# Branch projections of a hybrid decoder block: 512-column products over both parts of y_a and y_b, with the halves added per block

## The chip, the cores and the metric

The kernel runs on one core of one Trainium2 chip. The metric is the device time of one execution in microseconds (us), the median of several runs. A profile of one execution of the kernel before was recorded with it; times below that start at 0 count from the start of that profile's span.

## The reference

One layer of a hybrid decoder block over 256 tokens of width 1024, in float32. Two causal mixers (HGRN2, a gated linear recurrence, and MoBA, block-sparse attention, which with 256 tokens is one block and so plain causal attention) read the same projection of x; each gives an output of 8 heads x 128, y_a and y_b. These are projected by one 1024 x 1024 weight each, gated and summed, and projected once more. A SwiGLU feed-forward of width 2816 follows.

```python
proj = jnp.einsum('bsd,dn->bsn', x, w_in)
...
y_a = rms_norm(o_a, hgrn_norm_w...) * jax.nn.silu(hg...)
y_b = moba_attention(q_b, k_b, mv...)
z_a = jnp.einsum('bsc,cd->bsd', y_a, w_branch_a)
z_b = jnp.einsum('bsc,cd->bsd', y_b, w_branch_b)
g_a, g_b = jnp.split(jax.nn.sigmoid(gate_logits + b_gate), 2, axis=-1)
mixed = jnp.einsum('bsc,cd->bsd', g_a * z_a + g_b * z_b, w_out)
x = layer_norm(DN_ALPHA * x + mixed, ln1_w, ln1_b)
h = jnp.einsum('bsd,df->bsf', x, w_ffn_in)
h_gate, h_up = jnp.split(h, 2, axis=-1)
y = jnp.einsum('bsf,fd->bsd', jax.nn.silu(h_gate) * h_up, w_ffn_down)
return layer_norm(DN_ALPHA * x + y, ln2_w, ln2_b)
```

## The kernel before

**Products in two parts.** Every operand of a large product is split into two parts, each of TensorE's reduced fp32 type (fp32r): a leading part (an ACT copy that rounds, L156 for activations, L179 for weights) and the rest (a DVE subtraction, L157 and L181). A product is the sum of three: leading weights x leading activations, leading weights x rest, rest of weights x leading activations. The fourth is left out.

**Weights.** `plan()` lists 81 tiles of 1 MB in the order of use; `fetch()` gives the next tile as (wh, wl) and keeps three more on the way (`LOOKAHEAD`). Bringing a tile in is one DMA on SP's queue, the ACT cast (L179) and the DVE subtraction (L181). There are four buffers for leading parts (`whi`) and four for rests (`wlo`), so the cast of tile i + 4 waits until tile i has been used.

**Stages in order.** The input projections (hf, hq, hi, hg, gb, ga, mk, mq, mv), with the HGRN2 steps run between them; then `za` (four tiles of w_branch_a), with the attention of heads 4 to 7 between its matmuls; `zb` (four tiles of w_branch_b); `wo` (w_out), whose rows_pass takes the k-rows of m two at a time; the first layer norm with an early piece of the FFN (`fe`); the FFN's gate and up products (`fg`, `fu`); the down product (`wd`); the second layer norm.

**The branch projections.** `feat_pair` computes one weight tile's 256 output features for all 256 tokens into one accumulator (a PSUM tile of 2 x 256 columns from the pool `mm`, which has four). For each of the two 128-feature halves f and each of the eight k it issues three matmuls of 256 columns. One k is one head of y. y_a is held as two tiles, yah and yal; y_b as ybh and ybl. DVE then multiplies the accumulator by the gate (L539 for za; L546 for zb, after which L547 adds both branches and L156/L157 split the sum m into mTh and mTl).

**The attention heads.** `moba_head` is a generator: scores on PE (L487, L488), softmax on DVE and ACT (L491 to L500), then the transposes pt (L504), their copy pT (L506), the value product po (L509, L510), and the split into y_b (L156, L157). `side.step()` before each za tile issues one head's work, `side.drain()` the rest before zb.

**The FFN's form.** `wide_pair` (L686 on) already works with a `Pair`: a layout that keeps, for each k, the leading part and the rest side by side, so that both are one operand of 512 columns. It needs two accumulators per weight tile, one for each f; the left half collects leading x leading and rest x leading, the right half leading x rest. The two halves are then added: an ACT copy of the right half to SBUF (L712), and a DVE add of the left one (L713).

**The order.** Each engine runs its instructions in a fixed order, which a planner makes when the program is built (`schedule_with_timeline_sim=True`): it simulates the engines and takes, of the instructions that are ready in its simulated time, the one that comes first in the program. Only a few stretches (`manual_schedule`), wo and the FFN's early piece among them, keep the written order.

Of the kernel before, what the change touches and what calls it, by code (L numbers as in the profile page):

```python
# [10 lines left out]
F32 = mybir.dt.float32  # L11
F32R = mybir.dt.float32r
# [5 lines left out]
P = 128  # L18
T = 256
NT = T // P  # L20
D = 1024
KC = D // P
H = 8
# [87 lines left out]
def hybrid_layer_kernel(ctx: ExitStack, tc, x, xT, vecs, wts, ln1_w, ln1_b, ln2_w, ln2_b, consts, out):  # L111
    nc = tc.nc
# [6 lines left out]
    sm = pool("sm", 2)  # L119
    klp = pool("klp", 1)  # L120
    mm = pool("mm", 4, space=PSUM)
    aux = pool("aux", 4, space=PSUM)

    def slot(name, dt=F32):
        return big.tile([P, 2048], dt, tag="s8", name=name)
# [4 lines left out]
    class Pair:  # L130
# [6 lines left out]
        def __getitem__(self, key):  # L137
# [5 lines left out]
                ks = slice(k0, k0 + ks.stop - ks.start)  # L143
            return self.parts[i][:, ks, u, ts]

        def both(self, k):
            i, k = divmod(k, KC // 2)
            return self.parts[i][:, k, :, :]
# [6 lines left out]
    def split(dst_h, dst_l, src):  # L155
        nc.scalar.copy(dst_h, src)  # L156
        nc.vector.tensor_sub(dst_l, src, r32(dst_h))  # L157
# [27 lines left out]
    def fetch(ahead=LOOKAHEAD):  # L185
        while state["next"] < len(loads) and len(ready) < 1 + ahead:
            list(stage())
        return ready.pop(0)
# [36 lines left out]
    def feat_pair(name, ah=None, al=None):  # L225
        ah, al = (xTh, xTl) if ah is None else (ah, al)
        wh, wl = fetch()
        ps = mm.tile([P, 2, T], F32, tag="mm", name=name)
        for f in range(2):
            feat_steps(ps[:, f, :], wh, wl, f, ah, al, range(KC))  # L230
        return ps

    def feat_steps(ps, wh, wl, f, ah, al, ks, k0=0):
        wcol = slice(f * P, (f + 1) * P)
# [67 lines left out]
    for j in range(2, 4):  # L302
        ps = feat_pair(f"hf{j}")
# [4 lines left out]
    for j in range(4):  # L308
        ps = feat_pair(f"hq{j}")
        sg = sm.tile([P, 2, T], F32, tag="sg", name=f"sgq{j}")  # L310
        nc.scalar.activation(sg, ps, AF.Sigmoid)
        for f in range(2):
            h = 2 * j + f
# [3 lines left out]

    hv = slot("hv").rearrange("p (t d) -> p t d", t=NT)
    hgs = slot("hgs").rearrange("p (h t) -> p h t", h=H)
    yah = slot("yah", F32R).rearrange("p (h t) -> p h t", h=H)  # L320
    yal = slot("yal", F32R).rearrange("p (h t) -> p h t", h=H)

    def free_view(ap, offset, dims):
        return bass.AP(ap.tensor, ap.offset + offset, [ap.ap[0]] + dims)
# [9 lines left out]
    def hgrn_steps():  # L334
# [8 lines left out]
        for g in range(4):  # L343
            ps = aux.tile([P, 4, P], F32, tag="aux", name=f"sd{g}")
            cs = slice(g * 512, (g + 1) * 512)
# [8 lines left out]
        for l in range(LEVELS):  # L354
# [4 lines left out]
            for g in range(2):  # L359
                ps = aux.tile([P, 4, P], F32, tag="aux", name=f"sc{l}_{g}")  # L360
                for a in range(4):
                    h = 4 * g + a
# [25 lines left out]
        for g in range(2):  # L388
            for u in range(NT):
                ps = aux.tile([P, 4, P], F32, tag="aux", name=f"o{g}{u}")  # L390
                for a in range(4):
                    h = 4 * g + a
                    hd = slice(h * P, (h + 1) * P)
                    if u == 1:
                        nc.tensor.matmul(ps[:, a, :], SL[:, h, :], hv[:, 0, hd], start=True, stop=False)
                    nc.tensor.matmul(ps[:, a, :], SD[:, u, h, :], hv[:, u, hd], start=(u == 0), stop=True)
                sq = sm.tile([P, 4, P], F32, tag="sg", name=f"sq{g}{u}")
                nc.scalar.activation(sq, ps, AF.Square)
                st = sm.tile([P, 12], F32, tag="ost", name=f"ost{g}{u}")
                nc.vector.reduce_sum(st[:, 0:4], sq, axis=mybir.AxisListType.X)  # L400
                nc.vector.tensor_scalar(st[:, 4:8], st[:, 0:4], 1.0 / P, RMS_EPS, op0=ALU.mult, op1=ALU.add)
                nc.gpsimd.tensor_tensor(st[:, 8:12], st[:, 4:8], half, op=ALU.pow)
                dst = on[:, u, g * 512:(g + 1) * 512].rearrange("p (a d) -> p a d", a=4)
                nc.vector.tensor_tensor(dst, ps, st[:, 8:12, None].to_broadcast([P, 4, P]), op=ALU.mult)
            yield
            for j in range(2):
                h0 = 4 * g + 2 * j
                pt = aux.tile([P, 2, T], F32, tag="aux", name=f"ot{g}{j}")
                for a in range(2):
                    for u in range(NT):  # L410
                        hd = slice((h0 + a) * P, (h0 + a + 1) * P)
                        nc.tensor.transpose(pt[:, a, u * P:(u + 1) * P], on[:, u, hd], ident)
                ya = sm.tile([P, 2, T], F32, tag="sg", name=f"ya{g}{j}")
                nc.vector.tensor_mul(ya, pt, hgs[:, h0:h0 + 2, :])
                split(yah[:, h0:h0 + 2, :], yal[:, h0:h0 + 2, :], ya)
        yield

    class Steps:
# [49 lines left out]
    qT = slot("qT").rearrange("p (h t) -> p h t", h=H)  # L468
    kT = slot("kT").rearrange("p (h t) -> p h t", h=H)
    mv = slot("mv").rearrange("p (t d) -> p t d", t=NT)  # L470
    ybh = slot("ybh", F32R).rearrange("p (h t) -> p h t", h=H)
    ybl = slot("ybl", F32R).rearrange("p (h t) -> p h t", h=H)

    def rope_pair(nm, dst, j):
        ps = feat_pair(f"m{nm}{j}")
# [9 lines left out]
    def moba_head(h):  # L485
# [9 lines left out]
        p = s  # L495
# [12 lines left out]
        po = aux.tile([P, T], F32, tag="aux", name=f"po{h}")  # L508
        nc.tensor.matmul(po, mv[:, 0, hd], pT[:, 0:T], start=True, stop=False)  # L509
        nc.tensor.matmul(po[:, P:T], mv[:, 1, hd], pT[:, 2 * P:3 * P], start=False, stop=True)  # L510
        split(ybh[:, h, :], ybl[:, h, :], po)
        yield

    def moba_heads(h0):
# [19 lines left out]

    for j in range(4):
        side.step()
        ps = feat_pair(f"za{j}", yah, yal)
        cs = slice(2 * j, 2 * j + 2)
        nc.vector.tensor_mul(ga[:, cs, :], ps, ga[:, cs, :])  # L539
    side.drain()  # L540
    mTh = slot("mTh", F32R).rearrange("p (k t) -> p k t", k=KC)
    mTl = slot("mTl", F32R).rearrange("p (k t) -> p k t", k=KC)
    for j in range(4):
        ps = feat_pair(f"zb{j}", ybh, ybl)
        cs = slice(2 * j, 2 * j + 2)
        nc.vector.tensor_mul(gb[:, cs, :], ps, gb[:, cs, :])  # L546
        nc.vector.tensor_add(ga[:, cs, :], ga[:, cs, :], gb[:, cs, :])  # L547
        split(mTh[:, cs, :], mTl[:, cs, :], ga[:, cs, :])

# [136 lines left out]
    e[1][1].transpose()  # L686


    def wide_pair(name, p, tag):


        wh, wl = fetch()
        pss = []
        for f in range(2):
            ps = p.tile([P, 2, T], F32, tag=tag, name=f"{name}{f}")
            wcol = slice(f * P, (f + 1) * P)
            for k in range(KC):
                nc.tensor.matmul(ps, wh[:, k, wcol], x1p.both(k), start=(k == 0), stop=False)  # L698
                nc.tensor.matmul(ps[:, 0, :], wl[:, k, wcol], x1p[0, k, slice(0, T)],  # L699
                                 start=False, stop=(k == KC - 1))  # L700
            pss.append(ps)
        return pss

    room = slot("room").rearrange("p (i f t) -> p i f t", i=4, f=2)
    for j in range(EARLY, NF, 2):
        n = j // 2 % 2
        sums = []
        for i, (nm, p, tag) in enumerate([("g", mm, "mm"), ("u", aux, "aux")]):
            pss = wide_pair(f"f{nm}{j}", p, tag)
            s = room[:, 2 * i + n, :, :]  # L710
            for f, ps in enumerate(pss):
                nc.scalar.copy(s[:, f, :], ps[:, 1, :])  # L712
                nc.vector.tensor_add(s[:, f, :], ps[:, 0, :], s[:, f, :])  # L713
            if i == 0:
                nc.scalar.activation(s, s, AF.Silu)
            sums.append(s)
        nc.vector.tensor_mul(sums[0], sums[0], sums[1])
        i, k = divmod(j, KC)
        split(ah[i][:, k:k + 2, :], al[i][:, k:k + 2, :], sums[0])
# [46 lines left out]
```

## Time and profile before

| | |
|---|---|
| time, median of 3 runs | 513.84 us (513.62 to 514.0) |
| time of the profiled execution | 513.88 us |
| its span, first to last instruction | 511.8 us |
| mean granted TensorE clock | 0.998 |
| za matmuls: 64 each of L237, L238, L239 | mean 285, 288, 288 ns |
| zb matmuls: 64 each of L237, L238, L239 | mean 285, 283, 284 ns |
| weight cast L179 and subtraction L181 of one za tile | 1.90 and 2.29 us |
| HBM traffic over the span | 178 GB/s |

A row of a timeline gives the start in us from the span's start, the duration in us, the engine, the line of the kernel, the operation, what it writes and reads, the shapes, a count, and in brackets how long the engine had been idle before it and what ended that. PE is TensorE's matmul, PEld its weight load, DVE VectorE, ACT ScalarE, POOL GpSimd, SP the queue that issues the weights' DMAs. Matmuls overlap, so the duration of a row (0.28 us for 256 columns) is longer than the distance between the starts of two rows (0.12 us); where a stream's price is wanted, distances between starts are used. A row of a group gives the count, total busy time, the mean in ns, and the idle time before it.

### The profile page before, as it was taken

The page shows a single profiled execution, that of the slowest core. Times are in us where ns is not written, and L with a number is a line of the kernel's source. Part 1 is how long each engine was busy: PE and PEld are TensorE (multiplying, and loading weights), DVE is VectorE, ACT ScalarE, POOL GpSimd, SP SyncE. Part 2 cuts the span into 40 slices and gives each one's busy share as a digit, 9 for nine tenths or more (in the row PEclk, how much of TensorE's full clock was granted, in tenths as well). Part 3 has the DMA queues.
Part 4 walks back from the last instruction along what each step waited for, and adds up shares of the span by engine and source line. Part 5 has one row for each costly group of instructions (what it writes and reads, how often), then busy time and mean ns, then how long its engine had stood idle before and what let it go on. Part 6 is the DMA issues. An engine that isn't in the chain of part 4 may idle for free.

```text
span 511.8 us, 8120 instructions
## 1 busy us (share of the span) xinstructions
PE 501.4 (98%) x3440; PEld 467.3 (91%) x3440; DVE 338.5 (66%) x387; ACT 249.1 (49%) x303; POOL 39.9 (8%) x33
## 2 busy tenths in 40 slices
PE   8999999999999999999999999999999999999994
PEld 7899889999999998998999988998888888888884
DVE  5677799997565454776764799555756665643436
ACT  6695354444355445566552553444656556434300
POOL 0000000000020063352010000000000000000000
PEclk9999999999999999999999999999999999999999
DMA  7978544343424445543567276147555455437002
GB/s 247 374 280 311 184 172 158 106 150 156 165 83 165 167 169 197 198 161 118 227 214 279 104 269 239 48 165 246 166 193 218 165 181 218 178 122 257 32 1 82
DMA packets 15571, 91.70 MB, mean 179 GB/s; under 512 B 1840, under 2 KB 2864, under 8 KB 5552
## 3 DMA queue, kind: packets, MB, share of 16 engines
q1 hardware_dynamic: 14688, 88.04, 47.4%
q0 software_dynamic: 848, 3.15, 1.8%
q8 instruction: 27, 0.44, 0.3%
q14 instruction: 8, 0.07, 0.0%
HBM read 90.13 MB, written 1.05 MB: 178 GB/s over the span
## 4 chain that ended last, share of the span: by engine, by line
PE 94%; DMA 3%; DVE 1%; SPq 1%; ACT 0%; issue 0%; DVEq 0%
PE fg L698 6%; PE fu L698 6%; PE wd L567 4%; PE wd L566 4%; PE wd L568 4%; PE fu L699 3%; PE fg L699 3%; DMA raw<-in_wts_dram 3%; PE sc L363 3%; PE mk L239 2%; PE hq L239 2%; PE hq L238 2%; PE hq L237 2%; PE zb L239 2%; PE za L239 2%; PE mk L238 2%
## 5 line engine op out<-in xcount | busy, mean ns | idle before, releaser
L181 DVE TENSOR_TENSOR wl<-raw,wh 128x2048 fp32r<-128x2048 f32 (+2 forms) x88 | 186.5, 2122 | 121.1 <-ACT wh L179 120.8
L179 ACT CAST wh<-raw 128x2048 fp32r<-128x2048 f32 (+2 forms) x88 | 155.8, 1774 | 147.9 <-PE wd L568 18.4
L698 PE MATMUL fg<-x1p,wh 128*128 128x512 f32 x144 | 50.4, 392 | 0.0
L698 PE MATMUL fu<-x1p,wh 128*128 128x512 f32 x144 | 50.4, 392 | 0.0
L699 PE MATMUL fg<-x1p,wl 128*128 128x256 f32 x144 | 40.3, 280 | 0.0
L699 PE MATMUL fu<-x1p,wl 128*128 128x256 f32 x144 | 40.3, 280 | 0.0
L567 PE MATMUL wd<-wl,ah 128*128 128x512 f32 (+1 forms) x110 | 38.2, 348 | 0.0
L568 PE MATMUL wd<-wh,al 128*128 128x512 f32 (+1 forms) x110 | 38.1, 347 | 0.0
L566 PE MATMUL wd<-wh,ah 128*128 128x512 f32 (+1 forms) x110 | 38.0, 347 | 0.0
L698 PEld LDWEIGHTS fg<-x1p,wh 128*128 128x128 f32 x144 | 26.9, 187 | 5.9
L698 PEld LDWEIGHTS fu<-x1p,wh 128*128 128x128 f32 x144 | 26.9, 187 | 5.9
L699 PEld LDWEIGHTS fg<-x1p,wl 128*128 128x128 f32 x144 | 27.2, 189 | 0.0
L699 PEld LDWEIGHTS fu<-x1p,wl 128*128 128x128 f32 x144 | 27.2, 189 | 0.0
L566 PEld LDWEIGHTS wd<-wh,ah 128*128 128x128 f32 x110 | 20.8, 189 | 2.8
L568 PEld LDWEIGHTS wd<-wh,al 128*128 128x128 f32 x110 | 20.8, 189 | 2.6
L567 PEld LDWEIGHTS wd<-wl,ah 128*128 128x128 f32 x110 | 20.8, 189 | 2.5
L239 PE MATMUL hf<-xTh,wl 128*128 128x256 f32 x64 | 18.6, 291 | 1.4 <-DVE wl L181 1.3
L237 PE MATMUL hf<-xTh,wh 128*128 128x256 f32 x64 | 18.3, 286 | 0.9 <-ACT wh L179 0.9
L239 PE MATMUL za<-yah,wl 128*128 128x256 f32 x64 | 18.5, 288 | 0.0
L238 PE MATMUL za<-yal,wh 128*128 128x256 f32 x64 | 18.4, 288 | 0.0
L237 PE MATMUL hg<-xTh,wh 128*128 128x256 f32 x64 | 18.4, 288 | 0.0
L237 PE MATMUL mk<-xTh,wh 128*128 128x256 f32 x64 | 18.3, 286 | 0.0
(218 smaller groups left out, 1387.5 us busy)
## 6 DMA issues: line engine op xcount, KB each, us to landing
raw<-in_wts_dram SPq DMA_DIRECT2D x78, 1024.0 KB, 4.8
raw<-in_wts_dram SPq DMA_DIRECT2D x8, 256.0 KB, 4.7
xTr<-in_xT_dram SPq DMA_DIRECT2D x8, 128.0 KB, 4.6
raw<-in_wts_dram SPq DMA_DIRECT2D x2, 512.0 KB, 6.4
xr<-in_x_dram POOLq DMA_DIRECT2D x1, 1024.0 KB, 5.4
wb<-in_ln_w_dram POOLq DMA_DIRECT2D x2, 512.0 KB, 6.0
wb<-in_ln_b_dram POOLq DMA_DIRECT2D x2, 512.0 KB, 7.9
out_dram<-y SPq DMA_DIRECT2D x4, 256.0 KB, 2.1
```

Of the source, the lines that this page charges most:

```text
L179: nc.scalar.copy(h[:, ks, :], raw[:, ks, :])
L181: eng.tensor_sub(l[:, ks, :], raw[:, ks, :], r32(h[:, ks, :]))
L237: nc.tensor.matmul(ps, wh[:, k, wcol], ah[:, kk, :], start=(kk == 0), stop=False)
L238: nc.tensor.matmul(ps, wh[:, k, wcol], al[:, kk, :], start=False, stop=False)
L239: nc.tensor.matmul(ps, wl[:, k, wcol], ah[:, kk, :], start=False, stop=(kk == KC - 1))
L363: nc.tensor.matmul(ps[:, a, :], KL[:, h, :], later(Qt, n, h, 1), start=True, stop=True)
L566: nc.tensor.matmul(ps, lh(kk)[:, ts], wh[:, k, ns], start=(kk == 0), stop=False)
L567: nc.tensor.matmul(ps, lh(kk)[:, ts], wl[:, k, ns], start=False, stop=False)
L568: nc.tensor.matmul(ps, ll(kk)[:, ts], wh[:, k, ns], start=False, stop=(kk == ktot - 1))
L698: nc.tensor.matmul(ps, wh[:, k, wcol], x1p.both(k), start=(k == 0), stop=False)
L699: nc.tensor.matmul(ps[:, 0, :], wl[:, k, wcol], x1p[0, k, slice(0, T)], start=False, stop=(k == KC - 1))
```

## The change

y_a and y_b are held as `Pair`s (yap, ybp), and the za and zb loops use `wide_pair`, which now takes its operand as an argument and stands with the other helpers. For each half f and each k there is one matmul of 512 columns (leading weights, both parts) and one of 256 (rest of weights, leading part) in place of three of 256. The two halves of each accumulator are added by `add_halves` into a new SBUF tile z (pool `sm`, tag `sg`, two buffers), and the multiply by the gate reads z. The FFN's use of these helpers computes what it did.

```diff
+        def split(self, ks, src):
+            split(self[0, ks, slice(0, T)], self[1, ks, slice(0, T)], src)
...
+    def wide_pair(name, a, p, tag):
+        wh, wl = fetch()
+        pss = []
+        for f in range(2):
+            ps = p.tile([P, 2, T], F32, tag=tag, name=f"{name}{f}")
+            wcol = slice(f * P, (f + 1) * P)
+            for k in range(KC):
+                nc.tensor.matmul(ps, wh[:, k, wcol], a.both(k), start=(k == 0), stop=False)
+                nc.tensor.matmul(ps[:, 0, :], wl[:, k, wcol], a[0, k, slice(0, T)],
+                                 start=False, stop=(k == KC - 1))
+            pss.append(ps)
+        return pss
+
+    def add_halves(s, pss):
+        for f, ps in enumerate(pss):
+            nc.scalar.copy(s[:, f, :], ps[:, 1, :])
+            nc.vector.tensor_add(s[:, f, :], ps[:, 0, :], s[:, f, :])
...
-    yah = slot("yah", F32R).rearrange("p (h t) -> p h t", h=H)
-    yal = slot("yal", F32R).rearrange("p (h t) -> p h t", h=H)
+    yap = Pair("yap")
...
-                split(yah[:, h0:h0 + 2, :], yal[:, h0:h0 + 2, :], ya)
+                yap.split(slice(h0, h0 + 2), ya)
...
-    ybh = slot("ybh", F32R).rearrange("p (h t) -> p h t", h=H)
-    ybl = slot("ybl", F32R).rearrange("p (h t) -> p h t", h=H)
+    ybp = Pair("ybp")
...
-        split(ybh[:, h, :], ybl[:, h, :], po)
+        ybp.split(h, po)
...
-        ps = feat_pair(f"za{j}", yah, yal)
+        pss = wide_pair(f"za{j}", yap, mm, "mm")
+        z = sm.tile([P, 2, T], F32, tag="sg", name=f"za{j}")
+        add_halves(z, pss)
         cs = slice(2 * j, 2 * j + 2)
-        nc.vector.tensor_mul(ga[:, cs, :], ps, ga[:, cs, :])
+        nc.vector.tensor_mul(ga[:, cs, :], z, ga[:, cs, :])
...
-        ps = feat_pair(f"zb{j}", ybh, ybl)
+        pss = wide_pair(f"zb{j}", ybp, mm, "mm")
+        z = sm.tile([P, 2, T], F32, tag="sg", name=f"zb{j}")
+        add_halves(z, pss)
         cs = slice(2 * j, 2 * j + 2)
-        nc.vector.tensor_mul(gb[:, cs, :], ps, gb[:, cs, :])
+        nc.vector.tensor_mul(gb[:, cs, :], z, gb[:, cs, :])
...
-            pss = wide_pair(f"f{nm}{j}", p, tag)
+            pss = wide_pair(f"f{nm}{j}", x1p, p, tag)
-            for f, ps in enumerate(pss):
-                nc.scalar.copy(s[:, f, :], ps[:, 1, :])
-                nc.vector.tensor_add(s[:, f, :], ps[:, 0, :], s[:, f, :])
+            add_halves(s, pss)
```

More of the change, by code (lines that the diff above doesn't have):

```diff
@@ L686, in hybrid_layer_kernel @@
     e[1][1].transpose()
[L689 to L702, printed above, removed]
     room = slot("room").rearrange("p (i f t) -> p i f t", i=4, f=2)
```

## The prediction

> **What bounds the kernel now.** I read the page first (engines, then the chain of waits), then the busy time in stretches around the two branch projections, then the timelines of PE, DVE and ACT there.
>
> ```profile
> span 511.8 us, 8120 instructions
> PE 501.4 (98%) x3440; PEld 467.3 (91%) x3440; DVE 338.5 (66%) x387; ACT 249.1 (49%) x303; POOL 39.9 (8%) x33
> PE 94%; DMA 3%; DVE 1%; SPq 1%; ACT 0%; issue 0%; DVEq 0%
> ```
>
> PE is busy for 98% of the span, and 94% of the chain that ended last is PE. The profiled execution took 513.88 us by the clock, 2.1 us more than its span; the median of the three runs is 513.84, so what I take off the one I take off the other. The stretches (columns: length, then PE, PEld, DVE, ACT, POOL busy) are za with its attention heads, zb waiting for the last head, zb closing, and the first half of wo:
>
> ```profile
> 243.00:272.35 29.35, 29.35 (x236) 28.84 (x235) 19.11 (x38) 14.16 (x28) 3.13 (x5) 1.00 0.67 236
> 272.35:284.60 12.25, 12.25 (x104) 12.20 (x103) 3.74 (x4) 2.93 (x5) 0.00 (x0) 1.00 0.51 196
> 284.60:302.00 17.40, 17.40 (x125) 16.44 (x124) 16.55 (x17) 12.35 (x10) 0.00 (x0) 1.00 0.51 185
> 302.00:319.00 17.00, 17.00 (x80) 14.17 (x80) 16.29 (x17) 5.96 (x5) 1.00 (x1) 1.00 0.68 251
> ```
>
> PE has no gap in any of them, at a granted clock of 1.00. So time is won here only if the same sums need less PE time, and lost only if PE gets a gap it doesn't have. DVE is no reserve everywhere: 16.55 of 17.40 us while zb closes, but 3.74 of 12.25 just before.
>
> **The PE stream, removed and added.** A k-step of one 128-column half is three matmuls of 256 columns before, and one of 512 plus one of 256 after. The kernel already runs the second form in its FFN (L698, L699, moving x1p), with the same kinds of operands. Two uninterrupted stretches of the PE timeline:
>
> ```profile
> 246.87 0.28 PE L237 MATMUL za<-yah,wh 128*128 128x256 f32 x1
> 254.42 0.28 PE L237 MATMUL za<-yah,wh 128*128 128x256 f32 x1
> ...
> 355.95 0.39 PE L698 MATMUL fu<-x1p,wh 128*128 128x512 f32 x1
> 373.28 0.39 PE L698 MATMUL fu<-x1p,wh 128*128 128x512 f32 x1
> ```
>
> The first two rows are 21 steps apart: 7.55 / 21 = 0.3595 us a step. The last two are 50 steps apart: 17.33 / 50 = 0.3466. A step becomes 0.0129 us cheaper. There are 8 weight tiles x 2 halves x 8 k = 128 steps, so 1.65 us of PE disappear, half in za and half in zb. That is the whole of the gain, 0.32% of the time; a third of the weight loads goes too, but they ran beside the matmuls and are inside the two step prices.
>
> Here a rule of the Trainium skill speaks against the change. TensorE: Matmul & The Clock Gate, section Back-to-back issue gap, gives a warm matmul N/2.4 ns plus a fixed 2.5 ns; by it three matmuls of 256 are an estimated 327.5 ns and 512 plus 256 an estimated 325.0, so the 128 steps would save 0.32 us in place of 1.65. The trace differs from it (359.5 and 346.6 ns), and the trace decides.
>
> **The evacuation, added.** Each of the 16 accumulators gets an ACT copy of one half and a DVE add; the final multiply then reads z in place of the accumulator. The nearest rows are the same two instructions in the FFN, and multiplies with and without an accumulator operand:
>
> ```profile
> L712 ACT COPY room<-fg x18: 358/369/378, 346.6 to 440.0; 128x256 f32<-128x256 f32 x18
> L713 DVE TENSOR_TENSOR room<-fg,room x18: 412/416/418, 348.3 to 442.3; 128x256 f32<-128x256 f32 x18
> L546 DVE TENSOR_TENSOR gb<-zb,gb 128x512 f32<-128x512 f32 x4 | 2.7, 684 | 5.6 <-PE zb L239 5.6
> L547 DVE TENSOR_TENSOR ga<-ga,gb 128x512 f32<-128x512 f32 x4 | 2.8, 688 | 0.1
> ```
>
> So ACT gains 16 x 0.369 = 5.9 us and DVE 16 x 0.416 = 6.7 us, half in each projection, and the multiply stays at about 0.69. In za this lies beside PE: 3.3 us on a DVE that is free for 29.35 - 19.11 = 10.2 us, 3.0 on an ACT free for 15.2. It costs nothing while the accumulators come free in time. They come from a pool of four, and a tile now takes two where it took one, so an accumulator is needed again after one and a half tiles, 24 steps or 8.3 us, where before it was more than three tiles. In the FFN the interval from the last matmul to the end of the add, where neither engine is held up, is short:
>
> ```profile
> 354.44 0.28 PE L699 MATMUL fu<-x1p,wl 128*128 128x256 f32 x1
> 354.76 0.37 ACT L712 COPY room<-fu 128x256 f32<-128x256 f32 x1 [0.27 <-PE fu L699]
> 355.17 0.42 DVE L713 TENSOR_TENSOR room<-fu,room 128x256 f32<-128x256 f32 x1 [1.01 <-ACT room L712]
> ```
>
> That is 1.15 us. A weight cast of 1.9 us and a wl subtraction of 2.3 us queued ahead (rows below) make it 5.4, still under 8.3. A copy that waits for PE's tile holds up what is behind it on ACT (exps and pT copies of the heads, the next cast), and an add what is behind it on DVE (the heads' softmax, the next wl); PE waits for none of these soon, since casts run three tiles ahead. I cost za at nothing; without that cover it would be the excess over 8.3 us per tile.
>
> **The last head, moved.** The zb tiles run their steps for heads 0 to 6 while head 7 is still in its softmax. These rows follow head 7, from its transposes to the first use and the first finished tile:
>
> ```profile
> 272.35 0.28 PE L237 MATMUL zb<-ybh,wh 128*128 128x256 f32 x1
> 273.30 0.27 PE L504 MATMUL pt<-cst,ms 128*128 128x128 f32 x1
> 274.38 0.48 ACT L506 COPY pT<-pt 128x384 f32<-128x384 f32 x1
> 277.35 0.38 PE L509 MATMUL po<-pT,mv 128*128 128x256 f32 x1
> 278.61 0.42 DVE L157 TENSOR_TENSOR ybl<-po,ybh 128x256 fp32r<-128x256 f32 x1 [1.79 <-ACT ybh L156]
> 280.87 0.40 PE L237 MATMUL zb<-ybh,wh 128*128 128x256 f32 x2
> 284.55 1.91 ACT L179 CAST wh<-raw 128x2048 fp32r<-128x2048 f32 x1 [5.98 <-PE zb L238]
> 284.68 0.69 DVE L546 TENSOR_TENSOR gb<-zb,gb 128x512 f32<-128x512 f32 x1 [5.64 <-PE zb L239]
> ```
>
> zb starts at 272.35, head 7's y_b is split by 279.03, its wide partner k = 7 first runs at 280.87, and zb0 is only finished at 284.6: the planner, which fixes each engine's order when the program is built, has put some 30 steps of four zb tiles in front. After the change the pool holds two zb tiles, so only 2 x 14 = 28 steps can be done without head 7: 28 x 0.3466 = 9.70 us, about 10.7 with the transposes and value products of head 7 among them. Head 7 needs 279.03 - 272.35 = 6.68 us of that, and the cover is 4 us longer. What changes is the order: zb0 and zb1 now close one right after the other, at about 271.5 (272.35 less za's share) + 10.7 + 4 x 0.35 = 283.6, and zb2 can start only when zb0's first half has been copied and added, 1.15 us after the start of its last matmul. That matmul starts near 282.7, the add ends near 283.9. The bounds of this wait are 0 (head 7 closes zb0 earlier, as the data would allow) and 1.15; I take 0.1, by these rows.
>
> **The handover to wo.** After zb the rows of m = ga + gb are split and read by wo at once:
>
> ```profile
> 298.42 2.29 DVE L181 TENSOR_TENSOR wl<-raw,wh 128x2048 fp32r<-128x2048 f32 x1 [0.30 <-ACT wh L179]
> 300.63 1.29 DVE L157 TENSOR_TENSOR mTl<-ga,mTh 128x512 fp32r<-128x512 f32 x2
> 292.71 0.68 DVE L546 TENSOR_TENSOR gb<-zb,gb 128x512 f32<-128x512 f32 x1
> 296.35 0.40 PE L566 MATMUL wo<-wh,mTh 128*128 128x512 f32 x1
> 302.27 0.39 PE L568 MATMUL wo<-wh,mTl 128*128 128x512 f32 x1
> 304.99 0.39 PE L568 MATMUL wo<-wh,mTl 128*128 128x512 f32 x1
> ```
>
> The last two mTl are ready at 301.3 and 301.92; PE reads them at 302.27 and 304.99, so the slack is 1.0 and 3.1 us. The change puts 8 x 0.416 = 3.3 us more on DVE, wo starts 1.5 us earlier, and DVE's closing work starts 1.7 us earlier (283.0 for 284.68) or more: up to 3.1 us of slack goes. The later mTl then just holds; the earlier one holds only if it isn't queued behind the last wl, as it was. Bounds: 0 and 2.1 us. I take 0, because zb2 now closes near 289.4 where its multiply ran at 292.7, so its part is ready in time for the planner to place it ahead of that wl; and what PE consumes first is planned first.
>
> Weights, DMAs and the queues of SP and POOL are unchanged in number and order; the Pair layout takes two slots for y_a and two for y_b as the four tiles before did. The 1.65 us reach the end, since everything behind is the same PE stream.
>
> **The sum.** 513.88 - 1.65 + 0.1 = 512.3 us.
>
> **The rivals.** *DVE is late at wo.* For it: 16.55 of 17.40 us of DVE are taken in that stretch, and the earlier mTl stood behind a wl of 2.29. Against it: 8.5 us of idle DVE just before, which zb0's and zb1's adds can use. With 1.5 us of the 2.1 lost, 513.9 - 0.15 = 513.7, no measurable change.
>
> *PE runs out of open accumulators, slower.* Place: the end of head 7. Before, four open zb tiles covered it; now two. If the planner puts head 7's transposes and value product behind the 28 steps, or if za3 frees its pair late and only zb0's 14 steps (4.85 us) are there, PE waits for the round itself: 273.30 to 274.86 for transposes and copy, 277.35 to 279.03 for product and split, 1.56 + 1.68 = 3.24 us. Time: 513.88 - 1.65 + 3.24 = 515.5, and up to 516.6 with the 1.15 of the evacuation. It decides from the point where head 7 slips by more than the 4 us of cover; the added copies and adds sit on the engines that its softmax needs. Against it: the chain has only to keep its place, and value product and split stood 13 steps into zb.
>
> *Only columns count.* A step moves 768 columns before and after; if the FFN's 0.3466 owes its advantage to something else than the form (its operands, its place), nothing is saved: 513.9. The rule above would give 513.6 here. Against it: both stretches run at the full clock, without gaps, and each is long.
>
> **How the numbers follow.** A measurement of this kernel can tell about 0.2%, 1.03 us, from no change; so faster means under 512.8, slower over 514.9. My forecast (all stalls together under 0.6 us, 511.9 to 512.8) gets 0.54; DVE late at wo 0.20; accumulators run out 0.17; only columns 0.04; 0.05 is for a better case, with fewer switches between heads and projections, down to 511.7, and for mixtures, half of it faster. Faster: 0.54 + 0.03 = 0.57. Same: 0.20 + 0.04 + 0.01 = 0.25. Slower: 0.17 + 0.01 = 0.18. The range goes from 511.7 to 515.0: its upper end takes in the late wo (at its bound 514.3) and small shortages of accumulators, and leaves out most of that case. Signs are mixed, so the likeliest case's own range, 511.9 to 512.8, stands beside it.
>
> **What would show it.** Right: steps of za and zb at 0.347 us; 16 new copies of 0.37 and adds of 0.42; PE without a gap from 243 to 319; wo starting about 1.5 us earlier, near 294.9. Wrong: steps near 0.36 (only columns); in the list of waits, PE zb waiting for ybl or for an add in add_halves, near 277 to 285 (accumulators); PE wo waiting for mTl or wl near 300 (DVE). A shift of the same size with the FFN and later stages changed in length would mean that something outside these steps moved.

## The result, and the profile after

The changed kernel takes 519.86 us (median of 4 runs, 518.73 to 521.26) against 513.73 us before (4 runs): a ratio of 1.0119 [1.0105, 1.0134]. It is 6.1 us slower, where 512.3 was forecast; it lies above the range's 515.0 and above the slow rival's 516.6. One execution of a_za (617.8 us) and one of n_swap (1757.6 us), two experiments below, fell in a slow state and are left out of their times.

The profiled execution took 518.73 us, the shortest of the four. First its page and the four new lines in the list of PE's waits (total, times, longest, in us):

```profile
span 516.4 us, 7895 instructions
PE 502.1 (97%) x3312; PEld 461.1 (89%) x3312; DVE 343.7 (67%) x403; ACT 253.9 (49%) x319; POOL 39.8 (8%) x33
```

```profile
PE wo L593 <- DVE mTl L160: 1.8, 1, 1.8
PE wo L591 <- ACT mTh L159: 1.5, 1, 1.5
PE zb L245 <- DVE ybp L160: 0.9, 1, 0.9
PE zb L245 <- DVE zb L254: 0.9, 1, 0.9
```

There are 128 fewer matmuls, yet PE's busy sum rises by 0.7 us, in part because a row that stands behind a gap is drawn longer (0.50 us for 0.39 in the rows below); so a stream is better judged by its stages and by distances between starts. The stages by the starts of their first matmuls:

| stage | before, us | after, us | difference |
|---|---|---|---|
| za, with heads | 243.11 to 272.35: 29.24 | 242.16 to 269.65: 27.49 | -1.75 |
| zb | to 296.35: 24.00 | to 296.46: 26.81 | +2.81 |
| wo | to 319.03: 22.68 | to 323.57: 27.11 | +4.43 |

Together that is +5.49. The stages behind them kept their lengths, and za began 0.95 us earlier (the first stage, hf, waited 1.3 us for wl before, and did not in this execution). That leaves the 4.6 us by which the span grew; the median is 1.1 us above this execution, and no other execution has a profile. The two first rows of the table are not the worth of the form alone: head 6's transposes and value product, in za before, stand in zb now (273.14 and 276.28), which moves about 0.9 us from one row to the other. The same stretches of the windows view (length, then PE, PEld, DVE, ACT, POOL) show that PE now has gaps:

```profile
242.00:269.65 27.65, 27.65 (x165) 24.46 (x163) 20.09 (x40) 14.89 (x29) 3.04 (x5) 1.00 0.56 200
269.65:283.00 13.35, 12.43 (x75) 10.81 (x74) 5.38 (x12) 4.76 (x10) 0.00 (x0) 1.00 0.72 283
283.00:296.50 13.50, 12.58 (x72) 10.67 (x72) 11.57 (x14) 8.55 (x12) 0.00 (x0) 1.00 0.47 160
296.50:323.60 27.10, 23.81 (x107) 18.50 (x106) 24.02 (x29) 13.21 (x11) 1.00 (x1) 1.00 0.52 195
```

The granted clock is 1.00 in all four, and za has no gap. Its step is what was forecast: 20 steps from one row to the other, 6.94 / 20 = 0.347 us.

```profile
247.28 0.39 PE L245 MATMUL za<-yap,wh 128*128 128x512 f32 x1
254.22 0.39 PE L245 MATMUL za<-yap,wh 128*128 128x512 f32 x1
```

From here on a *gap* is how much later a matmul starts than the one ahead of it and the stream's usual distance (0.12 us behind 256 columns, 0.23 behind 512) would have it. Between 242 and 335 us the gaps of over 0.12 us add up to 0.36 us before and 6.4 after. Four rows hold 5.7 of them (1.09, 1.07, 1.92 and 1.65 us, at 282.49, 288.03, 304.62 and 308.67). Here are these and two others, picked from PE's timeline:

```profile
281.18 0.38 PE L531 MATMUL po<-pT,mv 128*128 128x128 f32 x2
282.49 0.50 PE L245 MATMUL zb<-ybp,wh 128*128 128x512 f32 x1 [0.92 <-DVE ybp L160]
284.03 0.51 PE L245 MATMUL zb<-ybp,wh 128*128 128x512 f32 x1
288.03 0.50 PE L245 MATMUL zb<-ybp,wh 128*128 128x512 f32 x1 [0.92 <-DVE zb L254]
304.62 0.50 PE L593 MATMUL wo<-wh,mTl 128*128 128x512 f32 x1 [1.75 <-DVE mTl L160]
308.67 0.50 PE L591 MATMUL wo<-wh,mTh 128*128 128x512 f32 x1 [1.50 <-ACT mTh L159]
```

The first is for head 7: its value product (po) stands right ahead of the k = 7 steps that need it, and all 28 covering steps have been run by then. One reason why head 7 is late is seen on DVE. In the changed kernel the subtraction of a weight tile stands ahead of head 7's first softmax step (second fence), before it stood behind (first fence). The next subtraction (271.67) then also comes ahead of its last softmax steps (274.94), where before only that of 267.62 did (270.02):

```profile
264.13 0.56 DVE L491 TENSOR_TENSOR ms<-s,cst 128x384 f32<-128x384 f32 x1 [1.27 <-PE s L488]
267.62 2.29 DVE L181 TENSOR_TENSOR wl<-raw,wh 128x2048 fp32r<-128x2048 f32 x1 [0.89 <-ACT wh L179]
```

```profile
264.81 2.29 DVE L184 TENSOR_TENSOR wl<-raw,wh 128x2048 fp32r<-128x2048 f32 x1 [2.12 <-ACT wh L182]
267.43 0.54 DVE L512 TENSOR_TENSOR ms<-s,cst 128x384 f32<-128x384 f32 x1
```

The second is for an accumulator. After the four k = 7 steps that close zb0 and zb1, zb2 starts at 284.03 in zb0's first accumulator, whose add ends at 283.97. Eight steps later it needs zb0's second one:

```profile
283.41 1.91 ACT L182 CAST wh<-raw 128x2048 fp32r<-128x2048 f32 x1
285.22 0.64 ACT L253 COPY zb<-zb 128x256 f32<-128x256 f32 x2
285.35 2.29 DVE L184 TENSOR_TENSOR wl<-raw,wh 128x2048 fp32r<-128x2048 f32 x1 [1.38 <-ACT wh L182]
287.56 0.75 DVE L254 TENSOR_TENSOR zb<-zb,zb 128x256 f32<-128x256 f32 x2
```

Its last matmul starts at 283.18, but its copy stands behind a cast and its add behind a subtraction, so it is free only near 288.0.

For wo (the third and the fourth gap), follow the last zb tile, whose matmuls end near 296.8. First ACT, then DVE:

```profile
296.59 3.72 ACT L182 CAST wh<-raw 128x2048 fp32r<-128x2048 f32 x2 [1.79 <-issue]
300.22 0.35 ACT L253 COPY zb<-zb 128x256 f32<-128x256 f32 x1
```

```profile
298.53 2.29 DVE L184 TENSOR_TENSOR wl<-raw,wh 128x2048 fp32r<-128x2048 f32 x1 [0.29 <-ACT wh L182]
300.74 0.68 DVE L572 TENSOR_TENSOR ga<-ga,gb 128x512 f32<-128x512 f32 x1
301.35 2.28 DVE L184 TENSOR_TENSOR wl<-raw,wh 128x2048 fp32r<-128x2048 f32 x1
303.55 0.41 DVE L254 TENSOR_TENSOR zb<-zb,zb 128x256 f32<-128x256 f32 x1
303.88 0.68 DVE L160 TENSOR_TENSOR mTl<-ga,mTh 128x512 fp32r<-128x512 f32 x1
304.48 0.68 DVE L571 TENSOR_TENSOR gb<-zb,gb 128x512 f32<-128x512 f32 x1
305.08 2.28 DVE L184 TENSOR_TENSOR wl<-raw,wh 128x2048 fp32r<-128x2048 f32 x1
307.29 0.68 DVE L572 TENSOR_TENSOR ga<-ga,gb 128x512 f32<-128x512 f32 x1
308.65 0.69 DVE L160 TENSOR_TENSOR mTl<-ga,mTh 128x512 fp32r<-128x512 f32 x1 [0.68 <-ACT mTh L159]
```

A copy of 0.35 us stands behind two casts (3.72 us). Its add stands behind two subtractions, the multiply behind the add, and the sum behind a third subtraction. That is the second wait of wo; the first is for zb2's mTl, at 303.88. Before, the chain was one multiply straight from the accumulator, and both last mTl were made at 300.63, ahead of two subtractions:

```profile
296.71 0.68 DVE L546 TENSOR_TENSOR gb<-zb,gb 128x512 f32<-128x512 f32 x1
301.84 4.49 DVE L181 TENSOR_TENSOR wl<-raw,wh 128x2048 fp32r<-128x2048 f32 x2
```

Now the first stands behind two and the second behind three.

### The profile page after: what moved, and what is told of

It reads as the page before. It is cut to its first block, busy times and chain, and to the rows that moved or that the text cites. A ratio compares the mean times of both kernels' runs of the same rounds, so it can differ in the third digit from the quotient of the medians.

```text
span 516.4 us, 7895 instructions
## 1 busy us (share of the span) xinstructions
PE 502.1 (97%) x3312; PEld 461.1 (89%) x3312; DVE 343.7 (67%) x403; ACT 253.9 (49%) x319; POOL 39.8 (8%) x33
## 4 chain that ended last, share of the span: by engine, by line
PE 94%; DVE 2%; issue 1%; ACT 1%; DMA 1%; DVEq 0%; SPq 0%
PE fu L245 6%; PE fg L245 6%; PE wd L592 4%; PE wd L593 4%; PE wd L591 4%; PE fu L246 3%; PE fg L246 3%; PE za L245 3%; PE sc L385 3%; PE zb L245 2%; PE hf L260 2%; PE hf L262 2%; PE hf L261 2%; PE mk L262 1%; PE hq L262 1%; PE hq L261 1%
## 5 line engine op out<-in xcount | busy, mean ns | idle before, releaser
L245 PE MATMUL zb<-ybp,wh 128*128 128x512 f32 x64 | 23.1, 403 | 1.8 <-DVE ybp L160 0.9
L245 PE MATMUL za<-yap,wh 128*128 128x512 f32 x64 | 22.9, 400 | 0.0
L261 PE MATMUL hf<-xTl,wh 128*128 128x256 f32 x64 | 18.7, 292 | 0.0
```

Of the source, the lines that this page charges most:

```text
L245: nc.tensor.matmul(ps, wh[:, k, wcol], a.both(k), start=(k == 0), stop=False)
L261: nc.tensor.matmul(ps, wh[:, k, wcol], al[:, kk, :], start=False, stop=False)
```

## The experiments

The theories, as the expectations number them. **1**: the loss lies in zb and at the handover to wo, from two accumulators per tile and from where copies, adds and weights stand in the order; **1a**: it is the order, not the amount. **2**: the extra ACT and DVE work costs time wherever it stands. **3**: copies and adds in za delay the heads. **4**: the hop over ACT, behind the casts. **5**: the adds, on a nearly full DVE. Unless said otherwise the data computed are those of the reference. "Narrow" is the form of before, three matmuls of 256 columns into one accumulator, reading the `Pair` layout.

### One projection at a time

```diff
 a_za, in the zb loop (b_zb: the same in the za loop)
-        pss = wide_pair(f"zb{j}", ybp, mm, "mm")
-        z = sm.tile([P, 2, T], F32, tag="sg", name=f"zb{j}")
-        add_halves(z, pss)
+        z = narrow_pair(f"zb{j}", ybp)
```

> Only za in the new form; zb goes back to three products of 256 columns per step with one accumulator per tile (from the Pair layout). Theory 1 (the 1.65 us of PE are won, half in za; all that is lost is lost in zb and at the handover to wo, through two accumulators per zb tile and through the order of copies, adds and weight work on ACT and DVE): about 0.8 us faster than before, 513.0, no wait of PE between 240 and 320. Theory 2 (the extra ACT and DVE work costs wherever it is, because it delays heads and weights): about half of the 6.1 us of loss, 516.8. Theory 3 (the head chain is delayed by the copies and adds in za, and PE waits for head 7): a PE wait for y_b near 281 remains, 514.

> Only zb in the new form; za with three products of 256 columns per step. Theory 1: the whole loss of the changed kernel and no gain from za, 519.9 + 0.8 = 520.7, with the same waits of PE in wo for mTl and mTh. Theory 2: half of the loss, 516.8. Theory 3: the PE wait for y_b near 281 is gone, the waits in wo stay, 519.8.

a_za took 515.22 us, 1.0028 [1.0018, 1.0038]; b_zb 520.26, 1.0117 [1.0097, 1.0138], before being 513.84. zb alone makes the whole loss, within the noise (about 1.6 us of b_zb's profile are due to a lower clock, see the last section). But za alone doesn't bring its 0.8 us either, although za itself has no gap: the loss is found later, in the waits of a_za:

```profile
PE wo L602 <- DVE mTl L160: 0.6, 2, 0.4
PE zb L257 <- ACT ybp L159: 0.5, 1, 0.5
```

Head 7 is late even for narrow zb tiles, so its delay comes from za (theory 3); the subtraction stands ahead of its first softmax step here too (265.22, then 267.83). In b_zb the wait for ybp is gone, as it should be, and those for the add, mTl and mTh are there (gaps of 1.12, 1.92 and 1.67).

### Without the evacuation, and with half of it

In d_noadd the multiply reads the left half of each accumulator, and the right half is left out of the sum. In e_copies the copies are made and not read. In g_adds there are no copies, and each add takes a constant table in place of the right half.

```diff
 d_noadd
-        z = sm.tile([P, 2, T], F32, tag="sg", name=f"zb{j}")
-        add_halves(z, pss)
-        nc.vector.tensor_mul(gb[:, cs, :], z, gb[:, cs, :])
+        for f in range(2):
+            c = 2 * j + f
+            nc.vector.tensor_mul(gb[:, c, :], pss[f][:, 0, :], gb[:, c, :])
 e_copies: as d_noadd, but with z, and ahead of each multiply
+            nc.scalar.copy(z[:, f, :], pss[f][:, 1, :])
 g_adds: as after, but in place of add_halves
+            nc.vector.tensor_add(z[:, f, :], pss[f][:, 0, :], cos)
```

> The whole change without the evacuation by halves: the gates multiply the left half of each accumulator directly, two multiplies of 256 columns for one of 512; the right half (leading weights x rest of y) is left out of the sum, and there are no copies and no adds. The matmuls and the two accumulators per tile are as in the change. Theory 1: what is left is the PE saving and at most the wait for head 7 (0.9): 512.1 to 513.0. If two accumulators per tile alone were the cause, the two waits in zb (about 2 us) would stay: 514. If the wide form in these loops were slower on PE itself: 516 or more.

> The whole change with its 16 ACT copies but without its DVE adds: the gates multiply the left half of each accumulator directly, as in d_noadd, and the copies of the right halves go to z, which nothing reads; so leading weights x rest of y is left out of the sum. Theory 4 (the hop over ACT is what costs: a copy stands behind a cast of 1.9 us on ACT, and the accumulator and DVE's next step wait for it): most of the loss is back, 517 to 519, with PE waiting for mTh or mTl in wo. Theory 5 (the adds cost, 16 x 0.42 us more on a DVE that is nearly full while zb closes): no loss, as d_noadd, 512.3.

> The whole change with its 16 DVE adds but without its ACT copies: each add takes the left half of the accumulator and a constant table in SBUF; the right half is left out of the sum and nothing waits for ACT. Theory 4: no loss, 512.3 to 513. Theory 5: the loss is back, 517 to 519, with PE waiting for mTl in wo.

| | us | ratio to before | over d_noadd | gaps, us |
|---|---|---|---|---|
| d_noadd | 512.27 | 0.9966 [0.9954, 0.9979] | | 0.36 |
| g_adds | 514.17 | 1.0009 [0.9999, 1.0018] | +1.9 | 1.64 |
| e_copies | 517.64 | 1.0070 [1.0055, 1.0085] | +5.4 | 4.65 |
| after | 519.86 | 1.0119 [1.0105, 1.0134] | +7.6 | 6.4 |

This separates the terms. d_noadd has the 512-column stream and two accumulators per tile, and it is 1.57 us faster than before: the saving is real and of the forecast size, and two accumulators per tile cost nothing while they are read straight away. In the windows of zb and wo PE has no gap:

```profile
269.65:283.00 13.35, 13.35 (x80) 11.74 (x79) 4.50 (x9) 4.12 (x8) 0.15 (x1) 1.00 0.80 301
283.00:296.50 13.50, 13.50 (x78) 11.82 (x77) 13.22 (x17) 7.99 (x6) 0.00 (x0) 1.00 0.50 171
296.50:323.60 27.10, 27.10 (x148) 23.52 (x147) 24.85 (x29) 10.17 (x9) 2.00 (x2) 1.00 0.59 226
```

DVE is busier here than in the changed kernel (13.22 for 11.57 us while zb closes), so a nearly full DVE alone makes no gap; but it leaves little room for the adds. The copies cost more than the adds although they are 5.9 us of an engine that is half idle. They are not read, and yet each multiply stands behind its copy: in e_copies' trace the first one in zb starts at 283.79, after the copy of 283.38, where d_noadd's starts as soon as its matmul is done. So e_copies measures the hop, not only 16 short copies. With the copies alone, zb waits twice and wo waits for mTl (gaps 1.08, 1.08, 1.57, 0.55). Two of the theories are thus each part of it, the hop over ACT (4) the larger.

### Another order

c_late moves the preparation of two FFN weight tiles behind the first layer norm. i_tail writes zb2 and zb3 into the stretch whose order is kept as written. f_aux takes zb2's accumulators from the other pool.

```diff
 c_late
-        prefetch(2)
         norm1(0)
+        prefetch(2)
 i_tail, at the head of the manual_schedule stretch
+        for j in range(2, 4):
+            branch_b(j)
 f_aux
-        pss = wide_pair(f"zb{j}", ybp, mm, "mm")
+        pss = wide_pair(f"zb{j}", ybp, *((aux, "aux") if j == 2 else (mm, "mm")))
```

> The whole change, and the two FFN tiles that are brought in during the first half of wo are brought in after the first layer norm's DVE work in the written order, so that two casts and two wl subtractions no longer stand ahead of the last copies, adds and splits of zb. Theory 1a (the order, not the amount, of the ACT and DVE work makes PE wait in wo): the waits for mTl and mTh, 3.3 us and their restarts, about 4.0, go: 516. Theory 2 (DVE has too much to do there in any order): the amount is the same, PE still waits in wo, or the layer norm and the FFN's first tile come late: 519 or more.

> The whole change, all sums as in it; the last two zb tiles stand inside the stretch that keeps the written order, ahead of the weights of wo and the FFN, so that ACT makes their copies before the casts that follow in the text, and DVE their adds before the wl subtractions. Theory 1a (the order makes PE wait in wo, 3.64 us of extra distance between starts plus restarts, and the FFN's weights have time): the waits in wo go and none appears in fe, unlike in c_late; the two waits in zb (1.09 and 1.07) stay: 519.9 - 4.2 = 515.7. Theory 2 (too much for DVE in any order): PE waits in wo or fe for as long as before, 519 or more.

> The whole change, all sums as in it; the third zb tile takes its two accumulators from the other pool, aux, so that three zb tiles can be open. If the pool of four is what makes PE wait in zb: both waits there (1.09 and 1.07 of extra distance between starts) go, as 42 steps can be done without head 7 and zb2 needs no accumulator of zb0; the waits in wo stay: 517.7. If the waits in zb come from the late head and the queues on ACT and DVE and not from the pool: they stay, 519.9.

c_late took 523.67 us, 1.0184 [1.0169, 1.0200]; i_tail 519.80, 1.0117 [1.0096, 1.0137]; f_aux 524.94, 1.0224 [1.0203, 1.0245]. None is better than the changed kernel, and each shows where its loss went. In all three a lower clock behind the gaps adds to it (last section): about 2.5, 1.6 and 1.9 us of the profiled executions. PE's waits of c_late:

```profile
PE fe L654 <- ACT x1p L159: 2.3, 1, 2.3
PE fe L655 <- DVE x1p L160: 2.1, 1, 2.1
PE wo L593 <- DVE mTl L160: 0.5, 1, 0.5
PE wo L591 <- ACT mTh L159: 0.4, 1, 0.4
```

In c_late, wo waits 0.9 us in place of 3.3: the weights standing ahead of mTh and mTl were indeed what made them late. But casts and subtractions then stand ahead of x1p, the last of these casts waits 6.93 us for its own DMA, and the FFN's early piece waits 4.4 us. In i_tail, with copies and adds ahead of the weights, wo waits for the weights (1.8 us for wl, 0.9 for wh). In f_aux both waits of zb are gone, as asked, and wo waits 8.9 us (4.5 for mTl, 4.4 for mTh). DVE has no free stretch from 297.5 to 307.5 us in the changed kernel (9.71 of 10 us busy), and in these three orders whatever is put first there makes something else late. Theory 1a in its simple form, that a better order alone would bring the time back, fell in these three forms.

p_dve puts the copies on DVE, which takes away the hop.

```diff
 p_dve
-            nc.scalar.copy(s[:, f, :], ps[:, 1, :])
+            nc.vector.tensor_copy(s[:, f, :], ps[:, 1, :])
```

> The whole change, all sums as in it, with the 16 copies on DVE in place of ACT: no hop between engines, but some 16 x 0.35 us more on DVE than in the changed kernel. Theory 4: most of the loss of e_copies (5.4 over d_noadd) goes, that of the adds (1.9) stays and DVE's extra 2.8 us in zb costs about as much as the adds there: 515 to 516. Theory 5 and 2 (DVE's amount decides): more than the changed kernel, 520 to 523.

It took 521.41 us, 1.0137 [1.0122, 1.0152]. The wait for zb0's second accumulator is gone, since a DVE copy doesn't queue behind casts; that for the first has a gap of 0.39, and those in wo are 1.84 and 2.79. Together with head 7's the four gaps are 6.1 us for 5.7. So the hop can be taken away without a gain; that the kernel is slower than with ACT is not shown to come from its waits, since a lower clock makes about 2.1 us of the profiled execution (last section).

### Freeing an accumulator earlier

At k = 7, n_swap issues the 256-column matmul ahead of the 512-column one. The sums are the same; but the weight buffer is then in use until the accumulator is done, and the copy can be planned ahead of the cast that waits for this buffer. n_swap2 is the same kernel, run once more. u_swap adds to it narrow za2 and za3; w_za01_zb1 makes za0, za1, zb0 and zb1 wide and the others narrow.

```diff
+                if k == KC - 1 and swap:
+                    nc.tensor.matmul(ps[:, 0, :], wl[:, k, wcol], a[0, k, slice(0, T)], start=False, stop=False)
+                    nc.tensor.matmul(ps, wh[:, k, wcol], a.both(k), start=False, stop=True)
+                    continue
```

> The whole change, all sums as in it; only at k = 7 of each half the matmul of 256 columns goes before the one of 512, so that the weight buffer is released no earlier than the accumulator is finished, and the planner puts each copy ahead of the cast that waits for that buffer. Theory 4 (the copies stand behind casts of 1.9 us): the copies run right after their matmuls, the second wait in zb (1.07) and most of the 4.0 in wo go, the wait for head 7 (1.09) stays: 515 to 516. If the hop over ACT is slow even with ACT free, or the order on DVE alone decides: 518 to 520.

> The kernel of n_swap once more, for its profile: the whole change with the last two matmuls of each half swapped, so that copies go ahead of casts. If the rest of the loss is the last head: a PE wait of about 1 us for y_b near 282, and a second one for the accumulators. If it is DVE's order while zb closes (three of the six wl subtractions stand ahead of the last splits): PE waits of 2 to 4 us for mTl in wo, with no cast between a matmul and its copy. Time as n_swap, 518.

> n_swap with za2 and za3 in three products of 256 columns: no added work on ACT and DVE while the last heads are in their softmax. If the delayed last head is the larger part of what n_swap still loses: 515 to 516, no wait for y_b. If the handover is: 518, with the waits in wo unchanged and only about 1 us less in zb (of which 0.4 is given back by the two narrow tiles).

> za0, za1, zb0 and zb1 in the new form, with the last two matmuls swapped; za2, za3, zb2 and zb3 in three products of 256. PE saving 64 x 0.0129 = 0.83 us. If only the added work of the closing tiles zb2 and zb3 makes PE wait in wo: no wait, 513.0. If the adds of zb0 and zb1 push the queue of DVE back as well: waits for mTl in wo, 514.5 to 516.

n_swap took 517.90 us (3 runs), 1.0075 [1.0058, 1.0092], and as n_swap2 518.54, 1.0091 [1.0078, 1.0104]; u_swap 517.52, 1.0065 [1.0051, 1.0080]; w_za01_zb1 517.23, 1.0067 [1.0050, 1.0084]. The copies do move: in n_swap2 those of zb0 run at 284.74, ahead of the cast at 285.27. In all of them zb's gaps shrink: from 1.09 and 1.07 to 0.63 and 0.39 in n_swap2, and to 0.39 alone in the two others, where za's last tiles are narrow and head 7 is in time. What remains is one wait of wo for mTl, 2.3 us in all three. It comes earlier than those of the changed kernel, at the second pair of k-rows, those of zb1. Here are w_za01_zb1's DVE rows (one row of 296.81 left out) and ACT rows:

```profile
292.20 1.28 DVE L592 TENSOR_TENSOR gb<-zb,gb 128x512 f32<-128x512 f32 x2
293.40 2.28 DVE L184 TENSOR_TENSOR wl<-raw,wh 128x2048 fp32r<-128x2048 f32 x1
295.60 1.28 DVE L593 TENSOR_TENSOR ga<-ga,gb 128x512 f32<-128x512 f32 x2
298.55 2.29 DVE L184 TENSOR_TENSOR wl<-raw,wh 128x2048 fp32r<-128x2048 f32 x1 [1.07 <-ACT wh L182]
300.76 0.68 DVE L593 TENSOR_TENSOR ga<-ga,gb 128x512 f32<-128x512 f32 x1
301.37 1.28 DVE L160 TENSOR_TENSOR mTl<-ga,mTh 128x512 fp32r<-128x512 f32 x2
```

```profile
296.61 1.91 ACT L182 CAST wh<-raw 128x2048 fp32r<-128x2048 f32 x1 [3.85 <-PE zb L262]
298.43 1.13 ACT L159 CAST mTh<-ga 128x512 fp32r<-128x512 f32 x2
```

Follow zb1. Before, its multiply ran at 289.31, its sum at 292.11, mTh at 292.82 and mTl at 296.11. Now its two adds end at 289.5, the multiply runs at 292.20 behind a subtraction, the sum at 295.60 behind the next, mTh at 298.43 behind a cast, and mTl at 301.37 behind a third subtraction. Each link has missed a place: 2.9 us late at the multiply, 3.5 at the sum, 5.6 at mTh, 5.3 at mTl. So a delay of a few us is passed on and can grow, although DVE idles 1.07 us on the way. An order that lets zb1's chain pass the weights here alone wasn't tried.

### Wide only where the evacuation has room

q_za01 uses the wide form for za0 and za1 alone, so that its copies and adds are over before head 7's softmax. q_za01d is the same with the copies on DVE.

```diff
-        pss = wide_pair(f"za{j}", yap, mm, "mm")
-        z = sm.tile([P, 2, T], F32, tag="sg", name=f"za{j}")
-        add_halves(z, pss)
+        if j in (0, 1):
+            pss = wide_pair(f"za{j}", yap, mm, "mm")
+            z = sm.tile([P, 2, T], F32, tag="sg", name=f"za{j}")
+            add_halves(z, pss)
+        else:
+            z = narrow_pair(f"za{j}", yap)
```

> Only the first two za tiles in the new form, with copies on ACT as in the change; za2, za3 and zb with three products of 256 columns. Their copies and adds are done by about 260, before the softmax of the last heads and long before zb closes. If the form is worth its PE saving where its evacuation has slack: 32 steps x 0.0129 = 0.41 us faster than before, 513.4, no PE wait from 240 to 320. If any added work on ACT and DVE delays the last head: PE waits for y_b near 281, 514 or more.

> As q_za01, with the four copies on DVE. If the evacuation has slack there, the engine of the copy is indifferent: 513.4. If DVE delays the heads: 514 or more, with a PE wait for y_b.

q_za01 took 513.27 us against 513.99 (12 and 23 runs), 0.9988 [0.9977, 0.9998]: no wait in zb or wo, and gaps of 0.4 us in all, as before. It is faster than both kernels, by a difference that the interval only just tells from none. q_za01d took 514.77, 1.0016 [1.0007, 1.0025]: the extra DVE work of two tiles, long before, comes out as two gaps at wo's mTl (0.41 and 0.55).

## Why the prediction was wrong

**The PE stream: right.** Steps at 0.347 us, and d_noadd measures 1.57 us for the forecast 1.65. The rival that only columns count is out. So is the estimate from the formula of the Trainium skill (TensorE: Matmul & The Clock Gate, section Back-to-back issue gap), which that page gives for an isolated matmul: it would save 0.32 us, a ratio of 0.9994, and d_noadd's interval ends at 0.9979.

**The evacuation, added: the step that failed.** Its durations were right (copies 0.36 us, adds 0.415), and za has no gap, as costed. What failed is the sentence that PE waits for none of the things held up behind a copy or an add soon, and with it the 8.3 us that an accumulator was given. Those are the rhythm of za, where accumulators close one after the other. In zb four of them close in four steps, and zb0's second one is wanted again 3.8 us after its last matmul starts (283.18, then 286.96). Its copy and add, with a cast and a subtraction ahead of them, took 4.8 us, less than the 5.4 that the prediction allowed for just that. Copies and adds were costed as work beside PE and held against free time per stretch and 8.3 us per accumulator. They are also positions in two fixed queues that hold the casts and subtractions of the weights, in an order that is planned anew. Measured by leaving them out they cost 7.6 us: 5.4 for the copies alone, 1.9 for the adds alone.

**The last head, moved: taken 0.1, measured 2.2.** The forecast wait is the one for zb0's first accumulator, and it came almost as described: last matmul at 282.82 (forecast 282.7), end of the add at 283.97 (283.9), start of zb2 at 284.03. These times are partly luck, since zb started 1.9 us earlier than assumed, and the wait for head 7 and head 6's matmuls in zb made up for it. The gap of 1.07 belongs to the second accumulator, which the prediction didn't follow. The other gap (1.09) is the cover itself. The prediction took head 7 to need 6.68 us from zb's start. It took 282.43 - 269.65 = 12.78, more than the 10.7 of cover: zb starts 2.7 us earlier than before, and head 7's split ends 3.4 later. That za's copies and adds sit on the engines of its softmax was named with the slow rival and given too little weight; a_za shows that delay without wide zb tiles.

**The handover to wo: taken 0, bound 2.1, measured gaps of 3.9.** (Two of 3.6 in sum, and two of 0.2 at 302.13 and 309.40.) The bound was too low. It counted DVE's added time against the slack of mTl, with DVE starting its closing work 1.7 us earlier. It started 1.1 us earlier (283.55 for 284.68) and idled again. Above all the bound left out that the last tile's copy can stand behind casts on ACT, and its add, multiply and sum behind subtractions on DVE, each a new place to wait in a chain that was a multiply and a sum. "What PE consumes first is planned first" did not hold.

**The rivals.** Both named the right places, and neither came true alone. *PE runs out of open accumulators* has the right mechanism (head 7's value product behind the 28 steps), but at a gap of 1.09 in place of 3.24, and the 1.07 beside it is for another accumulator than the one it priced at 1.15. *DVE is late at wo* has the right wait, at more than its bound of 2.1. Each was given a chance of its own, and both together only a part of 0.05; but one cause, new instructions in full queues, brings both: -1.65 + 2.2 + 3.9 = +4.5 of the +5.49 that the three stages grew, and the other 1.0 is in distances too small to list one by one.

## What to carry to other kernels

A change that shortens a full engine's stream and gives small instructions to half-idle ones is priced by where those stand in the queues, not by their durations: list for each new link (copy, add, then the reader) what stands ahead of it at the moment the full engine runs out of cover, and count that. To find out whether the saving or the side work decides, leave the side work out for one run: that showed a gain of 1.57 us and a cost of 7.6 in one comparison. Then use the new form only for those tiles whose result isn't needed soon; here that was worth 0.7 us (q_za01), just clear of nothing.

## What the hardware showed

A gap of PE can cost more than its length, and not in every execution. The granted clock is 1.00 or 0.50. In 16 profiles of this case (n_swap's has no clock record) it changes only on a grid of 3.41 us, whose place against the kernel differs from one execution to the next, and each drop behind a gap lasts one, two or three such windows (3.41, 6.83 or 10.24 us). Here are windows of that grid around almost the same gap at wo's mTl (2.44 and 2.41 us), first n_swap2, then w_za01_zb1; the figure after the POOL count is the granted clock:

```profile
300.26:303.67 3.41, 1.13 (x5) 0.61 (x4) 3.41 (x5) 1.96 (x2) 0.00 (x0) 1.00 0.36 94
303.67:307.08 3.41, 3.41 (x10) 2.63 (x9) 3.41 (x4) 2.42 (x2) 0.00 (x0) 0.50 0.63 262
```

```profile
297.68:301.09 3.41, 2.17 (x10) 1.44 (x8) 2.54 (x2) 3.41 (x4) 0.00 (x0) 1.00 0.64 264
301.09:304.50 3.41, 2.40 (x10) 1.99 (x11) 3.41 (x4) 2.70 (x3) 0.00 (x0) 1.00 0.72 250
```

In n_swap2 the gap lies in one window, PE is busy for 1.13 us of it, and the next window has half the clock: matmuls of 512 columns start 0.43 us apart in place of 0.23, which adds 1.6 us. In w_za01_zb1 the border of two windows cuts the gap, PE is busy for 2.17 and 2.40 us, and the clock stays. The 16 profiles have 2145 windows at full clock between 30 and 490 us. The six with PE busy for 1.59 us or less were all followed by half clock, those with 1.91 or more never; of three between, 1.66 and 1.80 were not and 1.89 was, so PE's busy time does not decide it alone. Without a profile the same shows in the mean clock: w_za01_zb1 took 516.0 to 516.6 us in the three executions with 0.998, and 517.9 to 518.9 in the three with 0.992 to 0.995. The Trainium skill (TensorE: Matmul & The Clock Gate, section What's actually happening) says that the clock is halved after an idle window of about 3.4 us, whose place in time doesn't follow the kernel. Length and free place agree; but the window need not be idle from end to end, as the 1.13 us show.

Half clock is not what made the changed kernel slow: its profile has none before 513.9 us, and the mean clock of its four executions is 0.996 to 0.998, within the 0.995 to 0.998 of the kernel before. It is a part of the time of seven experiments. The distances between starts that it adds sum up to 1.6 us each in the profiles of b_zb, i_tail, n_swap2 and u_swap, 1.9 in f_aux, 2.1 in p_dve and 2.5 in c_late.
